# The last modulation of the first layer: products on VectorE beside a feed-forward in place of matmuls in the mixing stage

## The chip, the core and the metric

The kernel runs on one core of a Trainium2 chip. TensorE multiplies matrices and writes PSUM (8 banks of 128x512 float32); VectorE (DVE) and ScalarE (ACT) work elementwise on SBUF and PSUM; GpSimd (POOL) does little here; SyncE (SP) issues most transfers from memory (HBM) to SBUF. Each engine executes its own instructions in order and waits on semaphores for the others. The metric is the device time of one execution in microseconds: 2349.34 us for the kernel before, the median of three runs (2348.81 to 2355.28).

## The reference

Two layers work on 512 tokens (256 of context, 256 latent) of width 1024. Each layer is a feed-forward, a mixing stage of four parallel branches (a state-space branch S5, two attentions, a gated recurrence) merged by gates, and a second feed-forward. Each of these three is modulated by vectors that depend on the conditioning alone:

```python
mod_lat = (silu(c) @ w_ada[layer] + b_ada[layer]).reshape(b, 1, 9, 1024)
mod_ctx = (silu(c_ctx) @ w_ada[layer] + b_ada[layer]).reshape(1, 1, 9, 1024)

def ffn_sublayer(x, mod, j, g_pre, g_post, w1, w3, w2):
    h = rms_norm(x, g_pre) * (1 + mod[3*j + 1]) + mod[3*j]
    return x + 0.5 * mod[3*j + 2] * rms_norm((silu(h @ w1) * (h @ w3)) @ w2, g_post)
```

So a layer has nine modulations of 1024 numbers for each of two conditioning vectors. Modulations 6, 7 and 8 of a layer belong to its second feed-forward: 6 and 7 (shift and scale) are needed when its input is normalised, 8 (the gate behind it) when its output is written. A modulation is a product of a 1024x1024 matrix (4 MB) with two vectors.

## The kernel before

**Layout.** Activations lie with the 1024 channels on partitions, as 8 blocks of 128 rows by 512 tokens. Weights come in pieces of 128x1024 float32 (512 KB). `piece` (L324) loads one into a raw buffer, and `split` (L315) makes of it two tiles of reduced mantissa: `whi` on ScalarE (L318) and the rest `wlo` on VectorE (L319). Each product is three matmuls: high times high, high times low, low times high (`mm3`, L346 to L348). There are 3 raw buffers (`wraw`) and 4 pairs of `whi` and `wlo` (`wsp`). So a fifth pair waits until TensorE has used up the first, and a load waits until a raw buffer is free.

**Feed-forward** (`ffn`, L665). The up half takes 44 pieces, two for each of 22 pairs. A pair fills two PSUM banks, 24 matmuls of 512 columns for each piece. Then `act` (L686 to L689) makes silu on ScalarE (`t`, from the first bank), the product `gf` on VectorE (with the second bank), its high part `gh` on ScalarE and the rest `gl` on VectorE. The banks `h13` come from a pool of four, which is two pairs: a pair's first piece waits for `t` of the pair two before, its second piece for that pair's `gf`. The second half (`down`) takes 22 pieces; its accumulators use the same four banks, and when one is finished `post_block` (L570) reads the gate modulation 3*s + 2.

**Modulations** are made in one of two ways.

- `ada_pe` (L435): 8 transfers of a weight block to a raw buffer (`araw`); for each, four matmuls of 32 rows by 256 columns in four column groups of the array (L443, tile `adaps`; the trace has two records for each); then an evacuation (`adaev`, L449), two transposes (`adat`, L452) and `modulation`.
- `ada` (L402): 8 transfers of a transposed weight block, for each four products with accumulation on VectorE (L425, `aj` or `araw` from `araw` and `cr`). `cr` is silu of a conditioning vector, repeated on all partitions (two loads and two activations on ScalarE for each half of the channels).

Both take the raw buffers that the weight pieces use, and SP issues their loads in the order of the program.

**What sets the order.** The program is written with Python generators. In a feed-forward, `pace` (L253) runs ahead of each weight piece and advances each generator of `self.beside` by its rate: 0.6 is three steps in five pieces. `ada` has 8 steps (one transfer each) for a modulation. `behind` (L267) gives a generator's instructions a priority 200 places later. A list scheduler of the language then fixes the order on each engine when the kernel is built. In the first layer's second feed-forward two generators run beside the pieces: the tables of the second layer's S5 branch (`s5_tables`: many small operations on VectorE, transposes `s5vt` and products `s5k` on TensorE) and modulations 0 to 2 of the second layer. In `mix`, `more` is such a generator as well: it is advanced while the attention (GQA) lane runs, one step for each step of a lane, and what is left is run at the end. The lanes alternate with gate projections (`pj`, 24 matmuls for each piece) and merges (`br`) from a list of fillers.

Of the kernel before, what the change touches and what calls it, by code (L numbers as in the profile page):

```python
# [27 lines left out]
ALL_T = (0, NTOK)  # L28
# [159 lines left out]
class Kern:  # L188
# [295 lines left out]
    def begin(self, lag=1, first=1, spread=3, early=0):  # L484
# [4 lines left out]
        m = self.mod[0][:2] = [self.cpool.tile([P, KB, 2], F32, name=f"mod0_{j}") for j in range(2)]  # L489
        H, ws, banks = self.new_h(), [], []  # L490

# [42 lines left out]
        for t in range(KB + lag):  # L534
# [7 lines left out]
            for half in hv:  # L542
                p, q = half[1]
                self.pre_block(0, 0, ob, H, half, rs[:, p:q])
            if first <= ob < first + 4:
# [3 lines left out]
            for i, w in enumerate(ws):  # L549
                for kb in range(ob + 1) if i == ob - first else (ob,):  # L550
                    c = slice(kb * P, kb * P + P)
                    self.mm3(banks[i], (w[0][:, c], w[1][:, c]), H[kb], kb == 0, kb == KB - 1)
            mark, tc.cur_priority = tc.cur_priority, now
        tc.cur_priority = mark
        return H, banks

    def pre_block(self, l, s, kb, H, half, rs):

        nc = self.nc
        v, (a, b) = half  # L560
        sh, sc = self.mod[l][3 * s], self.mod[l][3 * s + 1]
        hh, hl = H[kb]
        t = self.u("ht")
        nc.vector.scalar_tensor_tensor(
            t[:, a:b], self.x[kb][:, a:b], sc[:, kb, v : v + 1], rs, op0=ALU.mult, op1=ALU.mult)
        nc.scalar.activation(hh[:, a:b], t[:, a:b], AF.Identity, bias=sh[:, kb, v : v + 1])  # L566
        nc.vector.scalar_tensor_tensor(  # L567
            hl[:, a:b], t[:, a:b], sh[:, kb, v : v + 1], hh[:, a:b].bitcast(F32), op0=ALU.add, op1=ALU.subtract)
# [1274 lines left out]
    def run(self):  # L1843
        nc = self.nc
        self.setup()
        self.opt = [
            dict(plan=('H', 'h|GM', 'S'), rates=(1.5, 0.4, 1, 1, 1), share=0.75, pk='f', pv='a', pq='a', vtt='a', us='a', s1='f', sD='f', cap=18, gap=1),
            dict(plan=('H', 'h', 'G', 'M', 'S'), rates=(1.7, 1.3, 1.5, 1.5, 0.8), share=0, pk='a', pv='a', pq='a', vtt='f', us='a', s1='f', sD='f', cap=12, gap=2),
        ]

        H, banks = self.begin()
        self.gpre += self.vectors("norm_pre", 24, [1])
        self.gpost = self.vectors("norm_post", 24, range(DEPTH))
        self.mvec = self.vectors("mvec", 8, range(DEPTH))
        self.beside = [[self.ada(0, range(2, 6), False), 0.6, 0], [self.behind(self.s5_tables(0)), 0.6, 0]]
        W = self.A["ffn"]
        head = lambda l: [self.A["win"][l, i] for i in FIRST]
        H = self.ffn(0, 0, ALL_T, H, (0, 1), head(0), banks)
        self.finish()
        self.lower_bounds()  # L1860
        H = self.mix(0, ALL_T, H, (0, 2), (x for j in range(6, 9) for x in self.ada_pe(0, j)), [W[1, i] for i in range(self.start)])
        self.beside = [[self.behind(self.s5_tables(1)), 0.6, 0], [self.behind(self.ada(1, range(3), False)), 0.6, 0]]
        H = self.ffn(0, 1, ALL_T, H, (1, 0), [W[2, i] for i in range(self.start)])
        self.finish()
        self.beside = [[self.behind(self.ada(1, range(3, 9))), 0.9, 0]]
        H = self.ffn(1, 0, ALL_T, H, (1, 1), head(1), back=True)
        self.finish()
        H = self.mix(1, LAT_T, H, (1, 2), iter(()), [W[3, i] for i in range(4)])
        self.ffn(1, 1, LAT_T, H, None)
# [23 lines left out]
```

## Time and profile before

| | us |
|---|---|
| median of 3 runs | 2349.34 (2348.81 to 2355.28) |
| the profiled execution | 2359.76 |
| its span, first to last instruction | 2357.9 |
| TensorE busy | 2251.7 (95%) |
| VectorE busy | 1645.5 (70%) |
| ScalarE busy | 917.5 (39%) |

The stages of the first layer in the span: the first feed-forward from about 60 to 425 us, the mixing stage to about 985, the second feed-forward's up half to 1260, its second half to about 1400. The three modulations of `ada_pe` are made from 593 to 682 us.

In a row of a timeline the first number is the start from the span's begin, the second the duration; a bracket gives the idle time ahead and what ended it. Matmuls overlap, so the distance between starts tells more than a duration. A row of windows gives the stretch, its length, then the busy time of PE (matmuls), PEld (weight loads), DVE, ACT and POOL, each with its number of instructions, then the granted clock of TensorE (1.00 is 2.4 GHz), the share of the DMA engines and GB/s.

### The profile page before, as it was taken

Reading aid. Unit: us, or ns where it says so; the run is one execution under the profiler, and the core shown is the slowest. Engines: PE = TensorE matmul, PEld = TensorE weight load, DVE = VectorE, ACT = ScalarE, POOL = GpSimd, SP = SyncE. Lnnn points to the kernel's source line nnn. Section 1 sums busy time; section 2 is a strip of 40 time slices with the busy share of each in tenths; the row PEclk is TensorE's granted clock in tenths of the full one; section 3 lists DMA queues with packets and bytes.
Section 4 is the critical chain, followed back from the end, with each engine's and each line's share of the span. In section 5 each row is a group of like instructions: output and inputs, shape, how many; then the busy total and the mean of one; then the engine's idle time right before and its main releaser. Section 6 shows DMA issues by size and latency. Waiting matters only on the chain. (4 is left out here: it accounts for less than half of the span.)

```text
span 2357.9 us, 38834 instructions
## 1 busy us (share of the span) xinstructions
PE 2251.7 (95%) x15188; PEld 1887.3 (80%) x15188; DVE 1645.5 (70%) x4040; ACT 917.5 (39%) x1563; POOL 53.3 (2%) x116
## 2 busy tenths in 40 slices
PE   7999999999999999899999999999999989998998
PEld 4778779987567778888877898888898867888997
DVE  5886676756666584899865378777767776777554
ACT  3322323454444423532323333222335464445443
POOL 0000020000000000000002000000000000000000
PEclk9999999999999999999999999999999998998999
DMA  7545554221541153255554316566523431444654
GB/s 245 181 151 163 185 176 133 81 88 55 169 142 59 54 170 94 63 171 166 182 171 147 99 63 198 180 185 188 179 81 105 120 90 55 156 163 129 186 186 134
DMA packets 105270, 326.79 MB, mean 139 GB/s; under 512 B 16192, under 2 KB 17984, under 8 KB 105088
## 3 DMA queue, kind: packets, MB, share of 16 engines
q1 hardware_dynamic: 96448, 306.00, 42.1%
q0 software_dynamic: 4032, 9.93, 1.2%
q10 hardware_dynamic: 4608, 8.39, 1.0%
q8 instruction: 119, 1.95, 0.3%
q14 instruction: 63, 0.52, 0.1%
HBM read 311.20 MB, written 15.17 MB: 138 GB/s over the span
## 5 line engine op out<-in xcount | busy, mean ns | idle before, releaser
L318 ACT CAST whi<-raw 128x1024 fp32r<-128x1024 f32 x402 | 421.8, 1050 | 810.0 <-DMA raw<-in_ffn_dram 295.0
L319 DVE TENSOR_TENSOR wlo<-raw,whi 128x1024 fp32r<-128x1024 f32 x402 | 490.7, 1222 | 280.4 <-ACT whi L318 277.0
L346 PE MATMUL h<-hh,whi 128*128 128x512 f32 (+1 forms) x1472 | 527.8, 360 | 14.9 <-DVE gf L687 7.6
L348 PE MATMUL h<-hh,wlo 128*128 128x512 f32 (+1 forms) x1472 | 526.8, 359 | 8.6 <-DVE wlo L319 8.6
L347 PE MATMUL h<-hl,whi 128*128 128x512 f32 (+1 forms) x1472 | 526.1, 359 | 0.0
L346 PEld LDWEIGHTS h<-hh,whi 128*128 128x128 f32 x1472 | 281.9, 192 | 59.6 <-issue 7.9
L348 PEld LDWEIGHTS h<-hh,wlo 128*128 128x128 f32 x1472 | 281.9, 192 | 51.0 <-DVE wlo L319 8.8
L347 PEld LDWEIGHTS h<-hl,whi 128*128 128x128 f32 x1472 | 282.0, 192 | 38.8
L346 PE MATMUL pj<-hh,whi 128*128 128x256 f32 (+1 forms) x800 | 278.7, 350 | 4.6 <-ACT hh L566 3.1
L348 PE MATMUL pj<-hh,wlo 128*128 128x256 f32 (+1 forms) x800 | 275.9, 347 | 4.8 <-DVE wlo L319 4.8
L347 PE MATMUL pj<-hl,whi 128*128 128x256 f32 (+1 forms) x800 | 276.2, 347 | 0.8 <-DVE hl L567 0.6
L346 PE MATMUL y<-gh,whi 128*128 128x256 f32 (+1 forms) x726 | 241.0, 332 | 2.9 <-ACT t L686 2.5
L348 PE MATMUL y<-gh,wlo 128*128 128x256 f32 (+1 forms) x726 | 241.5, 333 | 0.0
L347 PE MATMUL y<-gl,whi 128*128 128x256 f32 (+1 forms) x726 | 240.9, 332 | 0.0
L346 PEld LDWEIGHTS pj<-hh,whi 128*128 128x128 f32 x800 | 155.0, 194 | 26.7 <-issue 6.4
L348 PEld LDWEIGHTS pj<-hh,wlo 128*128 128x128 f32 x800 | 154.5, 194 | 26.1 <-DVE wlo L319 5.9
L347 PEld LDWEIGHTS pj<-hl,whi 128*128 128x128 f32 x800 | 154.8, 194 | 19.0 <-issue 3.3
L346 PEld LDWEIGHTS y<-gh,whi 128*128 128x128 f32 x726 | 138.0, 190 | 16.4 <-ACT t L686 2.7
L347 PEld LDWEIGHTS y<-gl,whi 128*128 128x128 f32 x726 | 138.0, 190 | 12.9
L348 PEld LDWEIGHTS y<-gh,wlo 128*128 128x128 f32 x726 | 138.0, 190 | 12.8
L425 DVE SCALAR_TENSOR_TENSOR aj<-araw,cr 128x512 f32<-128x512 f32 x112 | 77.0, 687 | 59.7 <-DMA araw<-in_w_adaT_dram 59.7
L688 ACT CAST gh<-gf 128x512 fp32r<-128x512 f32 (+1 forms) x88 | 49.7, 565 | 145.6 <-DVE gf L687 145.4
(421 smaller groups left out, 3240.0 us busy)
## 6 DMA issues: line engine op xcount, KB each, us to landing
raw<-in_ffn_dram SPq DMA_DIRECT2D x267, 512.0 KB, 3.8
araw<-in_w_adaT_dram SPq DMA_DIRECT2D x104, 512.0 KB, 4.2
raw<-in_win_dram SPq DMA_DIRECT2D x102, 512.0 KB, 3.7
araw<-in_w_ada_dram SPq DMA_DIRECT2D x24, 512.0 KB, 4.1
raw<-in_wout_dram SPq DMA_DIRECT2D x17, 512.0 KB, 3.6
raw<-in_wbr_dram SPq DMA_DIRECT2D x16, 512.0 KB, 3.7
araw<-in_w_ada_dram SPq DMA_DIRECT2D x22, 256.0 KB, 5.4
s5G<-s5g POOLq DMA_DIRECT2D x16, 256.0 KB, 3.0
```

Source lines behind the costliest of these rows:

```text
L318: self.nc.scalar.copy(hi, src)
L319: self.nc.vector.tensor_tensor(lo, src, hi.bitcast(F32), op=ALU.subtract)
L346: mm(ps, wh, xh, start=start, stop=False, skip_group_check=True)
L347: mm(ps, wh, xl, start=False, stop=False, skip_group_check=True)
L348: mm(ps, wl, xh, start=False, stop=stop, skip_group_check=True)
L425: nc.vector.scalar_tensor_tensor(w if v else junk, w, 1.0, S[v], op0=ALU.mult, op1=ALU.mult, accum_out=t[:, 2 * op + i, v : v + 1])
L688: nc.scalar.copy(gh[:, a:b], gf[:, a:b])
```

## The change

Modulation 8 of the first layer leaves the generator that `mix` is given (which keeps 6 and 7) and stands ahead of the second layer's modulations 0 to 2, in one generator beside the first layer's second feed-forward. That generator's rate goes from 0.6 to 0.7.

```diff
@@ -1858,8 +1858,10 @@
         H = self.ffn(0, 0, ALL_T, H, (0, 1), head(0), banks)
         self.finish()
         self.lower_bounds()
-        H = self.mix(0, ALL_T, H, (0, 2), (x for j in range(6, 9) for x in self.ada_pe(0, j)), [W[1, i] for i in range(self.start)])
-        self.beside = [[self.behind(self.s5_tables(1)), 0.6, 0], [self.behind(self.ada(1, range(3), False)), 0.6, 0]]
+        H = self.mix(0, ALL_T, H, (0, 2), (x for j in (6, 7) for x in self.ada_pe(0, j)), [W[1, i] for i in range(self.start)])
+
+        mods = (x for g in (self.ada(0, [8], False), self.ada(1, range(3), False)) for x in g)
+        self.beside = [[self.behind(self.s5_tables(1)), 0.6, 0], [self.behind(mods), 0.7, 0]]
         H = self.ffn(0, 1, ALL_T, H, (1, 0), [W[2, i] for i in range(self.start)])
```

The order on each engine follows. TensorE, in the mixing stage where modulation 8 was made, before (`s` are scores, `ckt` and `cst` the recurrence, `hb` a broadcast of norms):

```order
L897 MATMUL s_6411<-dq_5073,dq_4941 128x256
L443 MATMUL adaps_6308<-araw_6435,cS 32x256 x3
L1151 MATMUL ckt_6441<-cst,ckd_6388 128x128 x3
L443 MATMUL adaps_6308<-araw_6457,cS 32x256 x4
L866 MATMUL hb_6853<-cst,ry_6840 128x128 x2
L443 MATMUL adaps_6308<-araw_6489,cS 32x256 x4
L1156 MATMUL cst_6447<-vc_4307,ckt_6442 64x64 x2
```

and now:

```order
L897 MATMUL s_6386<-dq_5073,dq_4941 128x256
L1151 MATMUL ckt_6410<-cst,ckd_6369 128x128 x3
L866 MATMUL hb_6794<-cst,ry_6781 128x128 x2
L866 MATMUL hb_6804<-cst,ry_6781 128x128 x4
L346 MATMUL pj_6531<-hh_3575,whi_6527 128x512
L347 MATMUL pj_6531<-hl_3576,whi_6527 128x512
L348 MATMUL pj_6531<-hh_3575,wlo_6528 128x512
L1156 MATMUL cst_6416<-vc_4307,ckt_6411 64x64 x2
```

The groups of `adaps` matmuls are gone, and a gate projection (`pj`), which stood further on, begins between the recurrence's transposes (`ckt`) and its state update (`cst`).

VectorE, in the second feed-forward, from `gf` of the 12th pair to that of the 13th, before:

```order
L687 TENSOR_TENSOR gf_10901<-t_10900,h_10875 128x512
L319 TENSOR_TENSOR wlo_11048<-raw_11045,whi_11047 128x1024
L689 TENSOR_TENSOR gl_10903<-gf_10901,gh_10902 128x512
L319 TENSOR_TENSOR wlo_11103<-raw_11100,whi_11102 128x1024
L425 SCALAR_TENSOR_TENSOR aj_10973,at_10974<-araw_10975,cr_10967 128x512
L425 SCALAR_TENSOR_TENSOR araw_10975,at_10974<-araw_10975,cr_10970 128x512
L425 SCALAR_TENSOR_TENSOR aj_10973,at_10974<-araw_10975,cr_10967 128x512
L425 SCALAR_TENSOR_TENSOR araw_10975,at_10974<-araw_10975,cr_10970 128x512
L425 SCALAR_TENSOR_TENSOR aj_10973,at_10974<-araw_11061,cr_10967 128x512
L425 SCALAR_TENSOR_TENSOR araw_11061,at_10974<-araw_11061,cr_10970 128x512
L687 TENSOR_TENSOR gf_11007<-t_11006,h_10981 128x512
```

and now the end of that stretch, which is 27 rows long, with 19 products (L425) and 5 `wlo` in it:

```order
L425 SCALAR_TENSOR_TENSOR araw_11119,mod_2_10534<-araw_11119,cr_10538 128x512
L425 SCALAR_TENSOR_TENSOR aj_10541,mod_2_10534<-araw_11119,cr_10535 128x512
L425 SCALAR_TENSOR_TENSOR araw_11119,mod_2_10534<-araw_11119,cr_10538 128x512
L319 TENSOR_TENSOR wlo_11161<-raw_11158,whi_11160 128x1024
L425 SCALAR_TENSOR_TENSOR aj_10541,mod_2_10534<-araw_11203,cr_10535 128x512
L425 SCALAR_TENSOR_TENSOR araw_11203,mod_2_10534<-araw_11203,cr_10538 128x512
L425 SCALAR_TENSOR_TENSOR aj_10541,mod_2_10534<-araw_11203,cr_10535 128x512
L425 SCALAR_TENSOR_TENSOR araw_11203,mod_2_10534<-araw_11203,cr_10538 128x512
L319 TENSOR_TENSOR wlo_11200<-raw_11197,whi_11199 128x1024
L687 TENSOR_TENSOR gf_10973<-t_10972,h_10947 128x512
```

Six products and two `wlo` stood between the two `gf`, and products of three more transfers have moved in.

VectorE further on, the last rows up to `gf` of the 19th pair, before:

```order
L319 TENSOR_TENSOR wlo_11670<-raw_11667,whi_11669 128x1024
L425 SCALAR_TENSOR_TENSOR aj_10973,at_10974<-araw_11854,cr_10967 128x512
L425 SCALAR_TENSOR_TENSOR araw_11854,at_10974<-araw_11854,cr_10970 128x512
L319 TENSOR_TENSOR wlo_11751<-raw_11748,whi_11750 128x1024
L425 SCALAR_TENSOR_TENSOR aj_10973,at_10974<-araw_11854,cr_10967 128x512
L425 SCALAR_TENSOR_TENSOR araw_11854,at_10974<-araw_11854,cr_10970 128x512
L319 TENSOR_TENSOR wlo_11790<-raw_11787,whi_11789 128x1024
L425 SCALAR_TENSOR_TENSOR aj_10973,at_10974<-araw_11936,cr_10967 128x512
L425 SCALAR_TENSOR_TENSOR araw_11936,at_10974<-araw_11936,cr_10970 128x512
L319 TENSOR_TENSOR wlo_11888<-raw_11885,whi_11887 128x1024
L425 SCALAR_TENSOR_TENSOR aj_10973,at_10974<-araw_11936,cr_10967 128x512
L687 TENSOR_TENSOR gf_11540<-t_11539,h_11514 128x512
```

and now, all from `gf` of the 18th pair:

```order
L687 TENSOR_TENSOR gf_11427<-t_11426,h_11401 128x512
L319 TENSOR_TENSOR wlo_11651<-raw_11648,whi_11650 128x1024
L689 TENSOR_TENSOR gl_11429<-gf_11427,gh_11428 128x512
L319 TENSOR_TENSOR wlo_11726<-raw_11723,whi_11725 128x1024
L425 SCALAR_TENSOR_TENSOR aj_11348,at_11349<-araw_11729,cr_11342 128x512
L425 SCALAR_TENSOR_TENSOR araw_11729,at_11349<-araw_11729,cr_11345 128x512
L687 TENSOR_TENSOR gf_11511<-t_11510,h_11485 128x512
```

The rest of the stream, which stood in front of this `gf`, now stands partly ahead of the 18th pair's `gf` (18 products since the 17th pair's) and partly behind this one. Up to the last `gf` of the up half there are 124 products, where there were 96.

## Rows read from the trace of the kernel before

**Rows 1.** The page: span, and busy time of each engine.

```profile
span 2357.9 us, 38834 instructions
...
PE 2251.7 (95%) x15188; PEld 1887.3 (80%) x15188; DVE 1645.5 (70%) x4040; ACT 917.5 (39%) x1563; POOL 53.3 (2%) x116
```

**Rows 2.** Windows by stage: span, busy us (instructions) of PE, PEld, DVE, ACT, POOL, clock, DMA.

```profile
655.00:685.00 30.00, 26.85 (x198) 15.22 (x197) 20.26 (x62) 13.53 (x31) 1.37 (x3) 0.94 0.52 159
685.00:985.00 300.00, 295.35 (x2093) 233.34 (x2093) 198.49 (x392) 124.93 (x224) 0.45 (x4) 1.00 0.31 96
...
1027.20:1260.40 233.20, 227.71 (x1120) 187.61 (x1118) 179.62 (x463) 70.34 (x94) 9.23 (x18) 0.99 0.56 175
```

**Rows 3.** Timeline of PE, mixing stage: start us, us, engine, line, operation [idle <-releaser].

```profile
660.44 0.64 PE L452 MATMUL adat<-cst,adaev 128*128 128x128 f32 x2 [1.59 <-DVE adaev L449]
661.01 1.94 PE L443 MATMUL adaps<-araw,cS 128*32 128x256 f32 x16
662.88 1.59 PE L924 MATMUL od<-p,vd 128*64 128x128 f32 x14
...
676.80 0.64 PE L443 MATMUL adaps<-araw,cS 128*32 128x256 f32 x8
677.37 0.43 PE L924 MATMUL od<-p,vd 128*64 128x128 f32 x2
...
679.49 0.44 PE L452 MATMUL adat<-cst,adaev 128*128 128x128 f32 x2 [0.60 <-DVE adaev L449]
679.68 0.47 PE L346 MATMUL pk<-bnh,mwh 128*64 128x512 f32 x1
```

**Rows 4.** Timeline of PE, late in the up half of the second feed-forward.

```profile
1228.11 0.39 PE L346 MATMUL h<-hh,whi 128*128 128x512 f32 x1
...
1233.32 0.39 PE L348 MATMUL h<-hh,wlo 128*128 128x512 f32 x1
1238.14 0.77 PE L346 MATMUL h<-hh,whi 128*128 128x512 f32 x1 [4.43 <-DVE gf L687]
...
1246.62 0.97 PE L1453 MATMUL s5k<-s5g,s5bd 128*32 128x112 f32 x32
```

**Rows 5.** Windows of 10 us there: the seventh number is PEclk, ahead of DMA.

```profile
1230.00:1240.00 10.00, 5.57 (x22) 4.25 (x21) 5.78 (x15) 2.62 (x3) 0.00 (x0) 0.87 0.49 158
1240.00:1250.00 10.00, 9.77 (x116) 7.72 (x115) 2.78 (x4) 2.34 (x4) 0.77 (x2) 0.79 0.39 104
```

**Rows 6.** Timeline of DVE, same place.

```profile
1215.76 0.69 DVE L425 SCALAR_TENSOR_TENSOR aj<-araw,cr 128x512 f32<-128x512 f32 x1 [1.93 <-DMA araw<-in_w_adaT_dram]
...
1218.46 1.22 DVE L319 TENSOR_TENSOR wlo<-raw,whi 128x1024 fp32r<-128x1024 f32 x1
...
1228.01 1.22 DVE L319 TENSOR_TENSOR wlo<-raw,whi 128x1024 fp32r<-128x1024 f32 x1
1234.09 0.69 DVE L425 SCALAR_TENSOR_TENSOR aj<-araw,cr 128x512 f32<-128x512 f32 x1 [4.85 <-DMA araw<-in_w_adaT_dram]
...
1237.30 0.69 DVE L687 TENSOR_TENSOR gf<-t,h 128x512 f32<-128x512 f32 x1
```

**Rows 7.** Timeline of SP, same place: the transfer's issue.

```profile
1229.26 0.33 SPq L421 DMA_DIRECT2D araw<-in_w_adaT_dram  x1
```

**Rows 8.** Timeline of DVE, a crowd of products between two gf.

```profile
1176.03 0.68 DVE L687 TENSOR_TENSOR gf<-t,h 128x512 f32<-128x512 f32 x1
...
1199.48 0.68 DVE L687 TENSOR_TENSOR gf<-t,h 128x512 f32<-128x512 f32 x1
```

**Rows 9.** Waits of PE, 60 to 300 us: us in total, times, longest.

```profile
PE h L346 <- DVE gf L687: 3.2, 1, 3.2
PE h L346 <- ACT t L686: 2.6, 3, 1.4
PE s5vt L1401 <- ACT s5vt L1402: 2.0, 1, 2.0
PE h L346 <- ACT whi L318: 1.7, 1, 1.7
```

## The prediction

> **What bounds the kernel now.** I read the page's busy shares first, then the windows by stage, then the timelines of the two places that the change touches. TensorE is busy 95% of a span of 2357.9 us [rows 1], so a change counts by what it does to TensorE: work taken off it, or waits put in front of it. The windows say where each can happen [rows 2]. In the mixing stage of the first layer TensorE is busy 26.85 of 30 us in the stretch that holds the last modulation (655 to 685), and 295.35 of 300 us behind it. In the feed-forward that follows, the stretch of its first half (two weight pieces for each pair of hidden blocks, 22 pairs) lasts 233.2 us; TensorE is busy 227.71 of them and VectorE 179.62. So VectorE has 53.6 us to spare there as a sum. Whether the sum can be used depends on its order, since it executes in order and TensorE waits for three things on it: `wlo` (L319) before a piece, `gf` (L687) before a PSUM bank is free, `gl` (L689) before the second half.
>
> One place shows what such a wait costs. TensorE issues its 24 matmuls of a piece evenly (23 intervals from 1228.11 to 1233.32, 0.2265 us each, 5.44 us a piece, 10.87 us a pair), then stops for 4.43 us until `gf` has executed, and needs from 1238.14 to 1246.62 = 8.48 us for the next piece [rows 4]. The granted clock of those two 10 us windows is 0.87 and 0.79 where 1 is the 2.4 GHz level [rows 5]: the engine came out of its stop at the lower level. So this stop costs 4.43 + (8.48 - 5.44) = 7.5 us. Its cause is on VectorE: the `gf` of 1237.30 stands behind a product with `araw`, which waited 4.85 us for its transfer [rows 6]; the transfer was issued at 1229.26 [rows 7], just when the `wlo` that started at 1228.01 had given its raw buffer back. Three raw buffers serve weights and modulations together.
>
> **Part 1: what leaves the mixing stage.** Eight transfers, 64 adaps matmuls in eight groups, one evacuation, two transposes. A group takes 0.57 us of TensorE's order (676.80 to 677.37), eight take 4.6; the two transposes 0.19 (679.49 to 679.68) and the wait ahead of them 0.60; the first two groups (661.01 to 662.88 = 1.87 us) hold 0.73 more than two times 0.57 [rows 3]. Together 6.1 us: the most that can come. The wait of 1.59 us at 660.44 stays, since it belongs to the modulation before. The least is not zero: in this stretch TensorE goes back and forth with VectorE and ScalarE (scores, softmax, transposes of the attention lane, the recurrence lane), and the adaps groups are its filler. The order of the changed kernel fills the holes from `ckt` on with gate projections (`pj`) that stood later; the first five groups lie ahead of that point and get no substitute, so five times 0.57 = 2.9 us of cover is gone there, and the pj matmuls that moved up are missing later beside the second attention lane. I bound the part by -6.1 and +2 us (the 2.9 and another stretch like it come back as waits while 3.9 of the work is all that leaves) and take -4.1: the work goes, about two thirds of the uncovered 2.9 come back as idle time. It is nearer to the low end because the 300 us behind this stretch are full [rows 2], so what is gained at its entry is not given back by a wait at its end.
>
> A rule of the Trainium skill speaks against this part. The rows: in 655 to 685 the weight loads (PEld) are busy 15.22 of 30 us, where the first half of the feed-forward has 187.61 of 233.2 [rows 2]. "Perfetto Trace Analysis", section "Identifying the Most-Contended Engine", says that matmul busy time is a poor measure of TensorE's distance from its limit and that the busy share of the weight loads is a better one. By it TensorE is half free in this stretch, the chain through VectorE is the bound, and Part 1 would be 0 instead of -4.1.
>
> **Part 2: what comes to VectorE beside the feed-forward.** Eight transfers of four products each: the four of 1215.76 end where the next operation starts, 1218.46, so 2.70 us a transfer [rows 6] and 21.6 us in all, with four more loads and activations of the conditioning vector on SP and ScalarE. The rate goes from 0.6 to 0.7 a piece, and by the order 124 products instead of 96 stand ahead of the last `gf`, which is seven transfers or 18.9 us: VectorE would be busy 198.5 us of some 226. As a sum it fits. The modulation is first read at the end of the first output blocks of the second half, and its products end ahead of the eighth of 22 pairs: no wait there.
>
> Locally it decides by how far `gf` of a pair comes behind. Four PSUM banks hold two pairs, so `gf` of a pair may come up to 10.87 + 5.44 = 16.3 us after its pair's last matmul, a little more where transposes of the state tables stand between. The old stop was the place with the last 11 products between two `gf`; in the new order only two stand there, and I take its 7.5 us as gone. Two new crowds stand earlier: 19 products and 5 `wlo` between `gf` of the 12th and 13th pair, 18 products, 3 `wlo` and four copies between the 17th and 18th. The densest of before without a stop had 14 products and 5 `wlo`, and took from 1176.03 to 1199.48 = 23.4 us [rows 8]; its work is 14 x 0.675 + 5 x 1.22 + 1.4 (`gf` and `gl`) = 17.0, so 6.4 us were waits for transfers and casts. The first new crowd is 19 x 0.675 + 5 x 1.22 + 1.4 = 20.3 of work and with the same waits 26.7; that is 15.8 more than a pair lasts, and with 1.9 for the `wlo` that stands ahead of a `gf` and the `gf` itself (1.22 and 0.69 in [rows 6]) 17.7: 1.4 us over the 16.3. The second comes to 12.2 + 3.7 + 1.4 + 6.4 and 1.4 for the four copies of half width, counted as two products, = 25.1, so 16.1: just under. So by this sum the new stops are 1.4 us; but the first feed-forward of the layer, the same kind of stage with the tables and a stream of modulations at 0.6, lost 3.2 + 2.6 + 2.0 + 1.7 = 9.5 us in its up half [rows 9]. I take 5.1, between the two, and Part 2 is -7.5 + 5.1 = -2.4 us. Its bounds are -7.5 (no new stop) and +15 (three stops like the old one, at both crowds and at the 20th pair, for one that goes).
>
> SP: the eight transfers move from behind the gate weights of the mixing stage, so those four loads come earlier, as the new order of pj needs; in the feed-forward they queue between weight pieces for the same three buffers, and that cost is in Part 2.
>
> **The sum.** -4.1 - 2.4 = -6.5 us on the profiled execution, 2359.76 us (its span and 1.9 us around it). That execution lies 10.4 us above the median of the runs shown, 2349.34, so some of its waits may be smaller in ordinary runs; I carry the difference over unscaled: 2349.34 - 6.5 = 2342.8.
>
> **Rivals.**
> 1. The filler was free. If the chain through VectorE sets the pace of 655 to 685, Part 1 is 0, and -2.4 is left: 2346.9. For it: the weight loads at half [rows 2], the wait of 1.59 us for `adaev` [rows 3]. Against: TensorE stood idle for only 3.15 of the 30 us, and the projections move up.
> 2. The old stop goes and no new one comes: -4.1 - 7.5 = -11.6: 2337.7. For it: both crowds come out within 1.4 us of what four banks allow. Against: the sister stage [rows 9].
> 3. Slower: VectorE's waits for transfers take over. The place is the two crowds and the 20th pair (where `gf` also stands behind a `wlo` that needs the piece before last); the price is 7.5 each as in [rows 4, 5], so 22.5 - 7.5 - 4.1 = +10.9: 2360.2. It decides once the waits exceed 6.4 - 1.4 = 5.0 us in the first crowd and 6.6 in the second; the old stop had 1.93 and 4.85 us [rows 6] in two of its waits alone. Against: the new crowds hold more work for VectorE between transfers, so a transfer has more time to land. The same page of the Trainium skill, section "Optimization Strategy", says that a gap that repeats on the saturated engine can mean too few buffers for the next tile; by that rule more transfers through three buffers bring more such gaps, and this rival would be the likeliest.
> 4. The change does nothing, the modulation being late or made twice: excluded by the order but for a slip, 2349.
>
> **How the numbers follow.** Chances: forecast 0.45 (own range 2336 to 2348), rival 1 0.17, rival 2 0.20, rival 3 0.15, rival 4 0.03. Within 0.3% (7 us), about what a measurement of this kernel tells from no change, lie a good half of the forecast, nearly all of rival 1 and rival 4: 0.44. Faster: nearly all of rival 2 and somewhat under half of the forecast with a little of rival 1: 0.42. Slower: rival 3 but for its mild end: 0.14. The range 2333 to 2354 takes in rival 2 with 5 us below it and the milder third of rival 3.
>
> **What would show it.** Right: no adaps groups between about 660 and 680, pj matmuls in their place, the mixing stage some 4 us shorter up to its last output projection; in the feed-forward no stop of 4 us in the 21st pair, and waits for `gf` or `t` of a few us in sum near the 13th to 20th pair. Wrong in Part 1: idle time of 4 us or more between 655 and 685 in TensorE's row, or a mixing stage as long as before. Wrong in Part 2: a window in the up half with a granted clock under 0.9 at the crowds, or the up half longer than 233 us. If ordinary runs of before lack the stop that the profile shows, the change comes out near 4 us or less.

## The result: 25 us slower, and the profile after

The changed kernel takes 2374.97 us (median of 6 runs, 2373.37 to 2384.70), the kernel before 2349.76 us in the runs beside it; the ratio is 1.010 with a 95% interval of 1.0081 to 1.0119. The forecast was 2342.8 us with a range of 2333 to 2354: wrong, and on the other side.

The page of the changed kernel, first lines [rows 1]:

```profile
span 2372.2 us, 38774 instructions
...
PE 2247.6 (95%) x15122; PEld 1884.9 (79%) x15122; DVE 1666.6 (70%) x4104; ACT 920.0 (39%) x1567; POOL 53.3 (2%) x116
```

TensorE has 66 instructions and 4.1 us of busy time less, and the span is 14.3 us longer than the one that the prediction started from. The busy share is 95% in both, so it tells nothing; the stages have to be compared. The table takes the start of a stage's first row in TensorE's timeline from the next one's: the mixing stage from its first `adaps` group to its last `cst`, its rest, then the up half (from the first `h` to the first `y`), and the second half. "Before again" is a second profiled execution of the kernel before, which ran at 2346.9 us; the runs beside it lie between 2346.27 and 2356.52 with a median of 2351.94, so it is a short one, as the first (2359.76) is a long one.

| us | mixing to last cst | rest of mixing | up half | second half | span |
|---|---|---|---|---|---|
| before | 83.1 | 315.0 | 270.3 | 125.4 | 2357.9 |
| before again | 83.1 | 315.1 | 263.8 | 125.3 | 2345.0 |
| changed | 91.5 | 314.8 | 276.4 | 131.0 | 2372.2 |

Both parts of the change lose: 8.4 us where modulation 8 left the mixing stage, and 18.3 us in the feed-forward against "before again" (11.8 against the execution of the prediction). Against "before again" the stages of the table hold 26.4 of 27.2 us; the rest is spread over the other stages.

**The mixing stage.** TensorE of the changed kernel there [rows 3]:

```profile
654.91 2.08 PE L866 MATMUL hb<-cst,ry 128*128 128x128 f32 x8 [3.79 <-DVE ry L297]
657.82 4.17 PE L843 MATMUL hs<-cst,bs 128*128 128x1 f32 x16 [0.84 <-DVE bs L1016]
663.59 0.69 PE L452 MATMUL adat<-cst,adaev 128*128 128x128 f32 x2 [1.59 <-DVE adaev L449]
...
669.80 0.77 PE L866 MATMUL hb<-cst,ry 128*128 128x128 f32 x2 [1.86 <-DVE ry L297]
...
678.16 1.16 PE L866 MATMUL hb<-cst,ry 128*128 128x128 f32 x8 [0.84 <-DVE m L900]
```

and VectorE of the changed kernel ahead of the first of these waits:

```profile
648.33 0.16 DVE L293 TENSOR_SCALAR ry<-rs 128x4 int32<-128x4 int32 x1
...
650.92 1.22 DVE L319 TENSOR_TENSOR wlo<-raw,whi 128x1024 fp32r<-128x1024 f32 x1
...
652.13 1.22 DVE L319 TENSOR_TENSOR wlo<-raw,whi 128x1024 fp32r<-128x1024 f32 x1
...
653.56 1.22 DVE L319 TENSOR_TENSOR wlo<-raw,whi 128x1024 fp32r<-128x1024 f32 x1
654.70 0.15 DVE L297 SCALAR_TENSOR_TENSOR ry<-rt,ry 128x4 f32<-128x4 f32 x1
```

`ry` is a chain of small operations (a reciprocal root in three rounds, L292 to L297) that TensorE waits for. Casts `wlo` of gate weights of 1.22 us each now stand between its links (these three, and one more ahead of the first row); before the change none did, and from L293 to the last L297 the chain took 3.6 us, where it now takes 6.4:

```profile
650.37 0.17 DVE L293 TENSOR_SCALAR ry<-rs 128x4 int32<-128x4 int32 x1
...
654.00 0.16 DVE L297 SCALAR_TENSOR_TENSOR ry<-rt,ry 128x4 f32<-128x4 f32 x1
```

The gate weights' loads come earlier because the eight modulation transfers that stood ahead of them are gone, and their casts come earlier with them. SP's issues of these loads, in the kernel before and in the changed one:

```profile
673.24 8.00 SPq L327 DMA_DIRECT2D raw<-in_win_dram  x4
```

```profile
639.94 15.20 SPq L327 DMA_DIRECT2D raw<-in_win_dram  x7
```

Granted clock of the changed kernel in three windows of 10 us (after the busy times; 1.00 is 2.4 GHz):

```profile
650.00:660.00 10.00, 5.38 (x22) 4.46 (x20) 5.46 (x14) 3.30 (x7) 0.00 (x0) 0.71 0.63 214
660.00:670.00 10.00, 6.55 (x29) 4.75 (x30) 5.95 (x26) 3.69 (x12) 0.53 (x1) 0.50 0.01 0
670.00:680.00 10.00, 9.16 (x38) 5.82 (x38) 5.83 (x16) 2.62 (x7) 0.84 (x2) 0.76 0.01 2
```

and of the kernel before in the middle one (1.00 in the two beside it):

```profile
660.00:670.00 10.00, 9.06 (x66) 4.61 (x67) 6.95 (x30) 4.27 (x12) 1.05 (x2) 0.83 0.55 163
```

The clock shares sum to 1.97 after and 2.83 before (2.66 in "before again", whose stage is as long). Within these windows the waits sum to 8.9 us after (the five brackets above) and 3.15 before. The two can't simply be added, since part of the slow clock passed while TensorE stood still anyway. The whole mixing stage, before and after, and then the stretch of the changed kernel at half clock, tell them apart:

```profile
593.41:991.50 398.09, 388.47 (x2987) 290.13 (x2986) 262.76 (x581) 170.42 (x329) 1.81 (x7) 1.00 0.36 111
```

```profile
590.69:997.00 406.31, 388.82 (x2920) 293.42 (x2920) 261.90 (x578) 170.39 (x329) 1.81 (x7) 0.97 0.32 99
654.28:674.76 20.48, 15.56 (x57) 11.37 (x58) 9.95 (x37) 5.36 (x15) 1.05 (x2) 0.50 0.23 81
```

Idle time (length less busy time) rose from 9.6 to 17.5 us, +7.9. TensorE was busy for 15.56 of the 20.48 us at half clock (0.50, 1.2 GHz). At full clock that work would take about half as long (the `pk` matmuls start every 0.43 us there, every 0.23 us at full clock), so some 7.8 us went there, an estimate. In the kernel before, the three windows amount to 3.4 us at half clock, all of it busy, and so to 1.7 us: +6.1. The matmuls that left are 5.5 us, the prediction's 6.1 without its wait of 0.60. Waits, clock and work: 7.9 + 6.1 - 5.5 = +8.5, against +8.2 measured for the whole mixing stage. The waits are the larger term, and the clock alone already takes back what the missing matmuls gained.

**The feed-forward.** Waits of TensorE in the changed kernel, 985 to 1300 us (us in total, times, longest) [rows 9 are the like of the first feed-forward]:

```profile
PE h L348 <- DVE wlo L319: 8.1, 4, 6.5
PE h L346 <- ACT t L686: 5.9, 2, 5.6
PE y L346 <- DVE gf L687: 3.9, 1, 3.9
PE h L346 <- ACT whi L318: 1.2, 2, 0.6
```

and in "before again", the same stretch:

```profile
PE h L348 <- DVE wlo L319: 6.5, 1, 6.5
...
PE h L346 <- DVE gf L687: 0.7, 1, 0.7
PE s5vt L1401 <- ACT s5vt L1402: 0.7, 1, 0.7
```

The wait of 6.5 us at the start of the stage is in both; the three others for `wlo`, 1.6 us, are new. The stop of 4.43 us that the prediction counted [rows 4] is 0.7 us in this execution of the same program. The new stop of 5.6 us, behind the 14th pair, is for `t` on ScalarE; timeline of ScalarE in the changed kernel:

```profile
1173.07 1.04 ACT L318 CAST whi<-raw 128x1024 fp32r<-128x1024 f32 x1 [3.26 <-DMA raw<-in_ffn_dram]
1175.66 1.04 ACT L318 CAST whi<-raw 128x1024 fp32r<-128x1024 f32 x1 [1.55 <-DMA raw<-in_ffn_dram]
1176.62 0.58 ACT L1402 COPY s5vt<-s5vt 128x512 f32<-128x512 f32 x1
1177.09 0.60 ACT L686 ACTIVATE t<-h 128x512 f32<-128x512 f32 x1
```

In ScalarE's order `t` of the 13th pair stands behind the casts of weight pieces up to the fourth after the 14th pair; two of these waited for their transfers. So TensorE stood still for a transfer that it did not need yet. VectorE was late there too: `gf` of the 12th and of the 13th pair, and the last matmul of the 13th pair:

```profile
1155.39 0.68 DVE L687 TENSOR_TENSOR gf<-t,h 128x512 f32<-128x512 f32 x1
...
1181.95 0.68 DVE L687 TENSOR_TENSOR gf<-t,h 128x512 f32<-128x512 f32 x1
```

```profile
1159.76 0.39 PE L348 MATMUL h<-hh,wlo 128*128 128x512 f32 x1
```

The two `gf` are 26.6 us apart, and the second ends 22.5 us after its pair's last matmul. TensorE needs it one piece (5.44 us) after it needs `t`; had `t` been in time, it would have waited some 5 us for this `gf` (an estimate from these rows). Its clock behind the stop:

```profile
1170.00:1180.00 10.00, 4.37 (x20) 3.50 (x19) 6.76 (x15) 3.08 (x4) 0.00 (x0) 0.83 0.71 232
1180.00:1190.00 10.00, 10.00 (x38) 8.09 (x37) 8.25 (x19) 2.16 (x3) 0.00 (x0) 0.83 0.34 110
```

The second stop is at the start of the second half, and has the form of the old one [rows 6]: VectorE's `gf`, which frees a bank, stands behind a product that waited 4.96 us for its transfer.

```profile
1276.71 0.69 DVE L425 SCALAR_TENSOR_TENSOR aj<-araw,cr 128x512 f32<-128x512 f32 x1 [4.96 <-DMA araw<-in_w_adaT_dram]
...
1278.47 0.68 DVE L687 TENSOR_TENSOR gf<-t,h 128x512 f32<-128x512 f32 x1
```

### The profile page after: what moved, and what is told of

Its sections match the earlier page's. It is cut to its first block, busy times and chain, and to the rows that moved or that the text cites. A ratio compares the mean times of both kernels' runs of the same rounds, so it can differ in the third digit from the quotient of the medians.

```text
span 2372.2 us, 38774 instructions
## 1 busy us (share of the span) xinstructions
PE 2247.6 (95%) x15122; PEld 1884.9 (79%) x15122; DVE 1666.6 (70%) x4104; ACT 920.0 (39%) x1567; POOL 53.3 (2%) x116
## 5 line engine op out<-in xcount | busy, mean ns | idle before, releaser
L347 PE MATMUL pj<-hl,whi 128*128 128x256 f32 (+1 forms) x800 | 274.8, 345 | 0.8 <-DVE hl L567 0.6
L347 PEld LDWEIGHTS pj<-hl,whi 128*128 128x128 f32 x800 | 153.5, 192 | 18.3 <-issue 2.5
L425 DVE SCALAR_TENSOR_TENSOR aj<-araw,cr 128x512 f32<-128x512 f32 x128 | 87.9, 687 | 53.9 <-DMA araw<-in_w_adaT_dram 51.5
```

What stands on the lines that cost most here:

```text
L347: mm(ps, wh, xl, start=False, stop=False, skip_group_check=True)
L425: nc.vector.scalar_tensor_tensor(w if v else junk, w, 1.0, S[v], op0=ALU.mult, op1=ALU.mult, accum_out=t[:, 2 * op + i, v : v + 1])
```

## The experiments

Times are medians, ratios are against the kernel before on the same chip, with their 95% intervals. The stages are those of each kernel's profiled execution:

| us | median | ratio | mixing to last cst | rest of mixing | up half | second half |
|---|---|---|---|---|---|---|
| mixing part alone | 2358.2 | 1.0020 to 1.0045 | 91.7 | 313.2 | 265.2 | 125.3 |
| + transfers | 2357.8 | 1.0016 to 1.0048 | 86.1 | 315.9 | 269.7 | 125.4 |
| + matmuls | 2358.8 | 1.0004 to 1.0037 | 90.2 | 312.5 | 266.2 | 125.4 |
| feed-forward part alone | 2365.7 | 1.0041 to 1.0065 | 83.0 | 315.2 | 274.9 | 129.6 |
| its products only | 2362.0 | 1.0022 to 1.0065 | 82.2 | 315.1 | 268.8 | 131.8 |
| its transfers only | 2361.4 | 1.0018 to 1.0041 | 82.6 | 315.1 | 274.8 | 125.7 |
| rate 0.6 | 2369.6 | 1.0047 to 1.0079 | 92.0 | 313.2 | 276.3 | 125.2 |
| rate 0.9 | 2373.6 | 1.0071 to 1.0118 | 90.7 | 313.7 | 278.2 | 125.4 |
| four buffers, changed | 2386.5 | 1.0125 to 1.0155 | 91.8 | 314.7 | 271.6 | 134.9 |
| four buffers, before | 2375.3 | 1.0076 to 1.0110 | 82.5 | 318.5 | 266.1 | 134.9 |
| smaller stream | 2352.1 | 0.9983 to 1.0006 | 82.6 | 315.2 | 262.2 | 125.3 |

A stage's time repeats well where its order is the same: the first column is 90.7 to 92.0 in all five kernels with the changed mixing stage and three raw buffers or four, 82.2 to 83.1 in all with the old one. The up half in the order of before is not so steady: 263.8 to 270.3 in five executions (before twice, and the first three rows above). The stretch ahead of the first `adaps` group (587.8 to 597.1 with three raw buffers) and the second layer's mixing stage (392.0 to 396.6, from the last `y` ahead of it to the first `h` behind it) vary too, which is why medians a few us apart don't separate kernels here. The stages in a row of the table are those of one execution; that of "+ matmuls" ran at 2350.4 us, the shortest of its ten.

**1. The kernel before again** (no edit).

> The kernel before once more, for a second trace: its profiled execution lay 10.4 us above the median of its runs. Theory: an ordinary execution lacks part of the half-clock time and the stop of 4.43 us in the 21st pair of the second feed-forward; expected 2347 to 2352 us with that stop gone or under 2 us. Rival: the stop is in every execution (its order is fixed) and the 10 us lie elsewhere.

2346.9 us, 0.1 below the expected range. The stop in the 21st pair shrank from 4.43 to 0.74 us without any change of the program: 6.5 of the 12.9 us between the two spans lie in the up half, 3.7 in the second layer's mixing stage, 2.7 ahead of 593 us. The first theory holds: the stop is not in every execution.

**2. The mixing part alone.** `(x for j in (6, 7) ...)`, and the gate takes modulation 2:

```diff
+        self.mod[0][8] = self.mod[0][2]
         self.beside = [[self.behind(self.s5_tables(1)), 0.6, 0], [self.behind(self.ada(1, range(3), False)), 0.6, 0]]
```

> Only the first half of the change: modulation 8 leaves the mixing stage and is made nowhere (its reader is given modulation 2 of the same layer, so that output is another one); beside the feed-forward the stream is as before, at 0.6. Theory A (the mixing stage itself became slower: wlo casts of gate weights stand inside the chain of the broadcast's reciprocal root, no filler covers the wait, and TensorE falls to half clock from 655 to 675 us): 2356 to 2362 us, +7 to +12 against before, with granted clock about 0.5 in two windows there. Rival B (the change's cost is all beside the feed-forward, the dip in the mixing stage being chance of one execution): 2345 to 2350 us.

2358.2 us, ratio 1.0032, and 91.7 us as in the changed kernel; theory A. The wait and the clock are there again:

```profile
PE hb L866 <- DVE ry L297: 5.6, 2, 3.8
```

```profile
660.00:670.00 10.00, 8.27 (x36) 6.36 (x36) 4.21 (x17) 3.04 (x9) 0.53 (x1) 0.50 0.07 24
```

**3. Transfers only, matmuls only**, both put back into experiment 2 as a third generator behind modulations 6 and 7:

```diff
...
+            nc.sync.dma_start(raw, self.A["w_ada"][l, j, kb])
+            nc.tensor.matmul(ps[:32, :16], self.cS[:, kb], raw[:, :16], start=kb == 0, stop=kb == KB - 1, skip_group_check=True)
```

```diff
...
+            for q in range(4):
+                nc.tensor.matmul(ps[32 * q : 32 * q + 32, :256], self.cS[:, kb], x, ...)
```

> As e1_mix_only (modulation 8 made nowhere), but the mixing stage still loads its eight blocks and reads 16 columns of each in one small matmul; the 32 matmuls are gone. In the order no wlo cast stands inside the chain of reciprocal roots. Theory A (the eight transfers kept the gate weights and so their casts out of that chain; the stop comes from the casts): the stretch from the first adaps group (593) to the last cst (676) takes 79 to 84 us as in the kernel before (83.1), not 91.7, and the whole 2345 to 2350. Rival B (the missing filler matmuls are the cause): 88 to 92 us there, 2354 to 2359.

> As e1_mix_only, but the 32 matmuls of modulation 8 stay in the mixing stage, on operands that lie in SBUF, without its transfers. In the order four wlo casts stand inside the chain as in the changed kernel. Theory A: the wait for ry of some 3 to 4 us stays; the filler behind it gives the clock back sooner; 86 to 92 us from 593 to 676, 2351 to 2358. Rival B (missing filler): 82 to 84 us there, 2346 to 2350.

Waits of TensorE for `ry`, 640 to 690 us, with the transfers, and then with the matmuls:

```profile
PE hb L876 <- DVE ry L297: 1.5, 1, 1.5
```

```profile
PE hb L878 <- DVE ry L297: 3.8, 1, 3.8
```

With the transfers the stop of 3.8 us is gone; with the matmuls it stays: the casts in the chain are its cause, and the missing transfers put them there. But the stage is back only to 86.1 and 90.2 us, not to 83.1; 86.1 lies between what the two theories forecast, so neither holds alone. The last `cst` does not stand at the same place in each order, so the two columns of the mixing stage have to be taken together: 404.9 us in experiment 2, 402.0 with the transfers, 402.7 with the matmuls, 398.1 before. Each half gives back 2.2 to 2.9 of 6.8 us. The granted clock of the three windows from 650 to 680 us is 0.90, 0.50 and 0.92 with the transfers and 0.57, 0.75 and 1.00 with the matmuls. Both sum to 2.32, between 1.98 in experiment 2 and 2.66 to 2.83 in the two executions of before. Only the sums compare: the second of these executions enters the stage 5.7 us earlier (587.8 against 593.5 us).

The whole times show neither gain: the medians of experiments 2 and 3 are 2358.2, 2357.8 and 2358.8 us, and the forecasts of 2345 to 2350 and 2351 to 2358 were missed. So the cause of the stop is shown; what stop and missing cover each cost rests on single executions.

**4. The feed-forward part alone.** The mixing stage of before, and `ada(0, [8], False)` beside the feed-forward, into the same tile:

```diff
-        new = {j: self.cpool.tile([P, KB, 2], F32, name=f"mod{l}_{j}") for j in js}
+        new = {j: self.mod[l][j] if self.mod[l][j] is not None else self.cpool.tile([P, KB, 2], F32, name=f"mod{l}_{j}") for j in js}
```

> Only the second half: the mixing stage makes modulation 8 with TensorE as before, and beside the feed-forward it is made once more on VectorE at 0.7 (into the same tile). Theory A: the stops for t in the 14th pair and for gf at the start of the second half remain as in the changed kernel, the mixing stage is as before: 2361 to 2366 us, +12 to +16. Rival B (all of the cost is here): 2372 to 2376. Rival C (nearly all is in the mixing stage): 2350 to 2355.

2365.7 us, +13.8, theory A. The two stops are those of the changed kernel:

```profile
PE h L346 <- ACT t L686: 5.2, 2, 5.0
PE y L346 <- DVE gf L687: 2.4, 1, 2.4
```

With experiment 2 (+6.3) that makes 20.1 of the 23 to 25 us.

**5. The rate**, 0.6 and 0.9 in place of 0.7 in the changed kernel:

```diff
-        self.beside = [[self.behind(self.s5_tables(1)), 0.6, 0], [self.behind(mods), 0.7, 0]]
+        self.beside = [[self.behind(self.s5_tables(1)), 0.6, 0], [self.behind(mods), 0.9, 0]]
```

> The changed kernel with the stream's rate at 0.6 as before, not 0.7. Theory A (three raw buffers carry too many transfers per pair; a slower stream leaves transfers time to land): 2364 to 2370 us, 5 to 11 less than the changed kernel's 2375, the gain all in the up half. Rival (the number of transfers decides, not their rate, or the order's accidents do): 2373 to 2380.

> The changed kernel with the stream's rate at 0.9, so that more transfers and products stand in each pair. In this order no t or gf stands behind the cast of the fourth piece ahead where TensorE has nothing else to do, but for the last pairs, which transposes and products of the tables cover. Theory A (places in the order make the stops): the stops for t in the 14th pair and for gf behind the up half go; 2356 to 2363 us. Rival (the three raw buffers or VectorE are overloaded; more per pair is worse): 2376 to 2390.

At 0.6 the time fell to 2369.6 as forecast, but the gain was in the second half (125.2), not in the up half (276.3). At 0.9 it was 2373.6, and theory A failed: the stop for `t` is gone as the order promised, but the up half is the longest of all, since TensorE now waits for casts whose transfers are late:

```profile
PE h L346 <- ACT whi L318: 7.3, 3, 2.5
```

In these three executions (0.6, 0.7 and 0.9) the rate decides which instruction waits and changes the up half by no more than 1.9 us.

**6. Products only, transfers only**, in experiment 4: the eight transfers left out (products on resident tiles), or each product cut to 16 columns.

```diff
+                    dry = (l, j) == (0, 8)
...
+                        w = S[i] if dry else raw[:, 512 * i : 512 * i + 512]
```

```diff
+                        n = 16 if (l, j) == (0, 8) else 512
+                        w = raw[:, 512 * i : 512 * i + n]
```

> As e2_beside_only, but the eight transfers of modulation 8 beside the feed-forward are left out; its 32 products run on tiles that lie in SBUF. From the 9th pair on the order is that of e2_beside_only. Theory A (the stop in the 14th pair comes from where the later stream stands at 0.7, not from the modulation's own transfers): the stop for t of about 5 us stays, 2358 to 2364 us. Rival (the eight added transfers through three raw buffers are the cause): no stop over 2 us there, 2350 to 2355.

> The complement of g1_products: as e2_beside_only, the eight transfers of modulation 8 stay beside the feed-forward, but each of its 32 products reads 16 columns in place of 512, so that VectorE's added work is nearly gone. Theory A (transfers and products each cost about half of the 11 us that e2_beside_only's up half lost): up half 267 to 272 us (e2_beside_only 274.9, the ordinary execution of before 263.8). Rival B (it is the transfers alone): 273 to 276. Rival C (VectorE's products alone): 262 to 266.

Products alone, and then transfers alone:

```profile
PE h L346 <- ACT t L688: 4.8, 2, 4.6
PE y L346 <- DVE gf L689: 3.6, 1, 3.6
```

```profile
PE s5vt L1402 <- ACT s5vt L1403: 6.4, 1, 6.4
PE h L346 <- DVE gf L688: 2.7, 1, 2.7
```

Without the transfers the two stops stay, because the order from the 9th pair on is the same (theory A), but the small waits ahead of them go: up half 268.8, 6.1 less than in experiment 4 and within what the kernel before has (263.8 to 270.3). With the transfers alone the up half is as long as with both (274.8), though the order and the stops are other ones; rival B there. The second half goes the other way: 131.8 us with the products alone, 125.7 with the transfers alone, 129.6 with both. So in these executions the length of the up half goes with the transfers, that of the second half with the products and their places in the order. The sums of up and second half are 400.6 and 400.5 with either and 404.6 with both, against 389.1 to 395.6 in five executions without; with that spread it can't be told whether the costs add.

**7. Four raw buffers**, in the changed kernel and in the one before:

```diff
-        self.slots = {t: pool("slot" + t, n) for t, n in (("u", 33), ("f", 22), ("h", 16), ("x", 8))}
-        self.wraw = pool("wraw", 3)
+        self.slots = {t: pool("slot" + t, n) for t, n in (("u", 31), ("f", 22), ("h", 16), ("x", 8))}
+        self.wraw = pool("wraw", 4)
```

> The changed kernel with four raw buffers in place of three (the room comes from two of the 33 work slots; the list scheduler then orders much of the program anew). Theory A (three raw buffers are what the added transfers run out of: the casts whi wait 87 us for transfers in the up half with the modulation and 65 without): the up half of the second feed-forward falls from 276 us to 264 to 268, the whole to 2358 to 2366. Rival (VectorE's added products and the order decide): the up half stays at 273 or more.

> The kernel before with four raw buffers and 31 work slots. Theory A: its up half has little to gain, 262 to 265 us against 264 in its ordinary execution; the whole within 5 us of before, below it if the first feed-forward's waits (9.5 us) go too. Rival: fewer work slots cost something, 2355 to 2365.

Both are much slower as a whole, and both forecasts of the whole were missed: the second half takes 134.9 us in both, 9.5 more. Its own products are not slower: the last `y` comes 123.8 us after the first in both, 125.3 in the kernel before. There the next stage's first matmul follows at once; in the new order it follows 11 us later, behind the sums of squares that its normalisation needs (kernel before with four buffers):

```profile
1394.73 1.87 PE L304 MATMUL st<-cst,sqa 128*128 128x1 f32 x8 [5.39 <-DVE sqa L587]
```

Whether that order comes from the two work slots or from the fourth buffer was not parted. The up half bears on the question: with the modulation it is 5.5 us longer than without (271.6 against 266.1), where three buffers gave 11.2 and 12.6 against "before again". What ScalarE's casts wait for transfers from 1010 to 1260 us, in the kernel before with four buffers, with three ("before again"; 69.5 in the first execution), in the changed kernel with four, and with three:

```profile
ACT whi L318 <- DMA raw<-in_ffn_dram: 16.6, 6, 4.9
```

```profile
ACT whi L318 <- DMA raw<-in_ffn_dram: 64.6, 22, 5.4
```

```profile
ACT whi L318 <- DMA raw<-in_ffn_dram: 61.1, 19, 7.1
```

```profile
ACT whi L318 <- DMA raw<-in_ffn_dram: 96.1, 32, 7.6
```

With a fourth buffer, in another order, the casts wait 35 to 53 us less. By the 5.5 us that the modulation still costs, about half of the up half's loss would be for want of a raw buffer. That share is not shown: against the first execution of before the changed kernel's up half loses only 6.1 us, and the fourth buffer comes with another order (theory A in part at most; its 264 to 268 us were not reached). Nor does the sum of these waits set the stage: at rate 0.6 it is 76.2 us and the up half as long as at 0.7, with four buffers it is 61.1 and the up half still 271.6.

**8. A smaller stream.** The kernel before with 16 transfers in place of 24 beside this feed-forward:

```diff
-        self.beside = [..., [self.behind(self.ada(1, range(3), False)), 0.6, 0]]
+        self.beside = [..., [self.behind(self.ada(1, range(2), False)), 0.45, 0]]
-        self.beside = [[self.behind(self.ada(1, range(3, 9))), 0.9, 0]]
+        self.beside = [[self.behind(self.ada(1, range(2, 9))), 1.0, 0]]
```

> The kernel before with a smaller stream beside the same feed-forward: modulation 2 of the second layer is made beside the next feed-forward (its stream goes from 0.9 to 1.0), the stream here goes from 0.6 to 0.45 and so from 24 transfers to 16. TensorE's order is word for word that of before. Theory A (transfers and products per pair set the stops): no stop in the 21st pair, up half 262 to 264 us in every execution, the next feed-forward as before to within 2 us; 2342 to 2348. Rival (the room in the next feed-forward is gone as it was in this one): its up half loses 5 us or more, 2350 to 2358.

The up half fell to 262.2 us, with no wait for `gf` in it:

```profile
PE h L346 <- ACT t L686: 0.2, 1, 0.2
```

and the casts wait for transfers 37.7 us. The stage came out as forecast in its one profiled execution, the whole (2342 to 2348) did not: it is the same as before (0.9983 to 1.0006), and what the up half gains is within what executions differ by elsewhere. None of these kernels beats the one before.

## Why the prediction was wrong

**Part 1, -4.1 us (bounds -6.1 and +2); measured +8.4.** The step that failed is the one on SP: "the eight transfers move from behind the gate weights of the mixing stage, so those four loads come earlier, as the new order of pj needs". It was costed at nothing (in the kernel before the transfers stood ahead of those loads, not behind them). Earlier loads brought earlier casts, and the list scheduler put these on VectorE into the chain that TensorE waits for. I showed TensorE's order of that place and not VectorE's, where the four casts could have been read. The second failure is the bound: idle time was counted at its own length, while [rows 5] already showed that a stop takes the clock down with it. Here the slow clock cost 6.1 us beside 7.9 us of waits. Rival 1 (the chain through VectorE sets the pace, Part 1 is 0) had the right picture and a wrong size: the chain did not stay as it was, it grew. The Trainium skill's rule behind it ("Perfetto Trace Analysis", section "Identifying the Most-Contended Engine") was the better guide: TensorE was far from its limit there, and taking work from it gained nothing.

**Part 2, -2.4 us (bounds -7.5 and +15); measured +11.8 against the same execution, 18.3 against "before again".** Three steps failed. First, the term of -7.5: the old stop was taken from one execution 10.4 us above the median, and most of it was not there in another (0.74 us); the text named this risk at its end but kept the term, and the 10.4 us were carried over as if they were everywhere alike. Second, the sum on how far `gf` comes behind had the crowds right (26.7 and 25.1 us forecast, 26.6 and 23.2 between the `gf` measured) but not the start: it let the 12th pair's `gf` come 1.9 us behind its pair, and that came 6.8 behind, so the 13th pair's came 22.5 us behind and not 17.7, 6.2 past the 16.3 and not 1.4. TensorE did not wait for it only because it already stood 5.6 us for `t`. That release, on ScalarE, was left out of the sum; ScalarE's order had to be read like VectorE's. Third, the price of the added transfers was looked for in the wrong place. "A transfer has more time to land" held for VectorE's products, but not for ScalarE's casts of weights. What the products wait for transfers in the up half, in "before again" (25.4 in the first execution) and in the changed kernel:

```profile
DVE aj L425 <- DMA araw<-in_w_adaT_dram: 22.0, 10, 4.7
```

```profile
DVE aj L425 <- DMA araw<-in_w_adaT_dram: 13.1, 9, 2.7
```

The casts, over the same stage, wait 96.1 us where they waited 69.0 and 73.9, and `t` stands behind them.

**The rivals.** Rival 3 (VectorE's waits for transfers take over, 2360.2) had the late transfers and the place of the first stop, but not the engine: in the up half VectorE's own waits for transfers fell. Its feed-forward price, 22.5 - 7.5 = +15, lies between the +11.8 and the 18.3, which is luck, since it is the price of three stops, of which only the first came; and it still held Part 1 at -4.1. The Trainium skill's sentence on too few buffers ("Perfetto Trace Analysis", section "Optimization Strategy"), by which this rival would have been the likeliest, is in accord with experiments 6 and 7 (up half 274.8 us with the transfers alone, 268.8 with the products alone; 61.1 us of waiting casts with four buffers, 96.1 with three), but how much of the loss it explains is not shown. Rival 2 fell. What would have shown each step wrong was named rightly: idle time of over 4 us between 655 and 685 (5.1), a clock under 0.9 at the first crowd (0.83), an up half over 233 us (239.4, from 1032.9 to 1272.3).

**What stays open.** Why the up half with the transfers alone loses as much as with transfers and products together is not settled: each variant has an order of its own, and the stop falls elsewhere in each. Nor was a kernel tried that keeps the old order of every engine and only makes a transfer late, which would part the two. In the mixing stage no kernel kept the casts out of the chain without the transfers. And the stages of each kernel come from one profiled execution, while the up half of the kernel before differs by 6.5 us between two.

## What to carry to other kernels

Work that is taken off the busiest engine is worth something only where that engine is the bound at that place. Where it waits for a serial chain, the work was a cover, and its transfers may have held back other work from that chain: read the new order of every engine that feeds the wait, not only of the one that is relieved. Count added loads against the buffers that they pass through and ask who stands behind a late one in each engine's order; spare time as a sum is no answer. And take no stop from a single execution as a term before a second one has shown it.

## What was not expected of the hardware

After waits of 3.79, 0.84 and 1.59 us, with work between them, the granted clock stayed at 0.50 for a whole window of 10 us and below 0.8 in the two beside it; matmuls were issued again in between. That is 20.5 us at half clock, and TensorE worked for 15.6 of them, which cost 7.8 us. Before the change, with fewer waits and filler groups behind them, the worst of the three windows was at 0.83 in one execution and 0.73 in the other, 3.4 and 6.8 us at half clock, though the order was the same in both, and the waits to 0.01 us (0.46 and 0.45, then 1.59 and 0.50). The Trainium skill says that TensorE's power scales with its use, so that matmuls should come back to back ("Perfetto Trace Analysis", section "Matmul Optimizations"); the clock fell furthest where the engine stood still most, which agrees.
